# Half as many one-hots on GpSimd, and one spread of expert numbers for all heads

## The chip, the cores and the metric

The kernel runs on one core of one Trainium2 chip. Times are microseconds (us) of the device for one execution; smaller is better. The core has five engines that run side by side, each through its own list of instructions in a fixed order: TensorE (PE in the profile; PEld is its loading of weights), VectorE (DVE), ScalarE (ACT), GpSimd (POOL) and SyncE (SP, which here only starts transfers). An instruction that waits for data holds up all that stands behind it on its engine. Transfers between the device's memory (HBM) and the core's memory (SBUF) run on 16 DMA engines. GpSimd's queue starts the gathers (transfers by index) and the stores of one-hot sums; SyncE's queue starts the rest.

## The reference, cut to what matters

One layer of a streaming encoder on 512 tokens of width 1024. The first sub-layer (attention, an mLSTM, branch gates) is not touched by the change. The second one picks 16 of 16384 single-neuron experts for every token and each of 8 heads:

```python
s = jnp.einsum("thpd,hpnd->thpn", q, sub_keys)
s_top, i_top = lax.top_k(s, PEER_TOPK)
cand = (s_top[:, :, 0, :, None] + s_top[:, :, 1, None, :]).reshape(PEER_BLOCK, PEER_HEADS, 256)
best, ci = lax.top_k(cand, PEER_TOPK)
i1 = jnp.take_along_axis(i_top[:, :, 0, :], ci // PEER_TOPK, axis=-1)
i2 = jnp.take_along_axis(i_top[:, :, 1, :], ci % PEER_TOPK, axis=-1)
e = i1 * N_KEYS + i2
gate = jax.nn.softmax(best, axis=-1)
act = jax.nn.gelu(jnp.einsum("thkd,td->thk", u_exp[e], xb))
return jnp.einsum("thk,thkd->td", (gate * act), v_exp[e])
```

So each token has 128 slots, each with a first expert number, a second one and a gate.

## The kernel before, in words

The 512 tokens are four chunks of 128. The experts of chunk 0 and of the first 32 tokens of chunk 1 are **gathered**: rows of u are fetched by expert number, a dot product with the token on VectorE gives the activation, and (chunk 0 only, in the last stage) rows of v are fetched and summed. All other tokens are done **densely**: for every one of 128 groups of 128 experts TensorE computes the hidden activations of 352 tokens (`hidden`, 24 matmuls from a 512 KB piece of u) and then, in `output`, adds them times v.

The dense way needs, for every token, a 128x128 matrix of gates by first and second number. `build` (line 778) makes it: for one token, `oa` is the one-hot of the first numbers times the gate, `ob` the one-hot of the second numbers, and one matmul `ps_g<-o,oa` (line 801) of the two gives the matrix. It goes in steps of four tokens (`t4`). Per step, `o4` (line 784, VectorE) holds all four `ob`; the four `oa` are shared out: `tt == 1` goes to GpSimd (line 799), `tt == 0` to ScalarE in two instructions (lines 795 and 796, from the 33rd token of chunk 1 on), also `tt == 2` in every fourth step, the rest to VectorE (line 799). ScalarE copies the four results to `gst` (line 802), and after eight steps GpSimd's queue stores 2 MB (`gd<-gst`, line 807). With chunks 2, 3 and 1, in this order, that is 96 steps and 12 stores.

`group` (line 714) serves the 32 gathered tokens of chunk 1. Head by head it forms the expert numbers `et` (line 723, VectorE), spreads them over the 128 partitions by four small transfers to `eg` on SyncE's queue (line 726), and then for four columns gathers a 512 KB tile `ur` of rows of u (line 704, GpSimd's queue) and takes the dot product `junk` (line 712, VectorE): 32 columns in all. `gathered` (line 742) does the same for chunk 0 with 128 columns. Five buffers `ur` are shared by all gathers.

`paced` (line 957) weaves these generators. While `build` takes a step, the side work advances by a rate: `RATE_B` = 0.4 of a `hidden`, `RATE_G` = 0.65 of a step of `group` while chunks 2 and 3 are built, `RATE_0` = 0.8 of a step of `gathered` while chunk 1 is. Between the last head of `scores` and the first build, `TOP` = 2 further `hidden` are called. `group` has a stop after every head's transfers and one after every column: 40 before its end. `slowly` adds that VectorE's part must not be placed ahead of the last `wlo` (line 150, the low half of a weight piece) traced so far.

The program order is not the final one: `schedule_with_timeline_sim` lets a planner simulate the engines with estimated costs when the program is built, and each engine's instructions are lined up as that simulation had them ready. That is why the first heads' `et` stands on VectorE beside the last heads of `scores`.

Of the kernel before, what the change touches and what calls it, by code (L numbers as in the profile page):

```python
# [14 lines left out]
I32 = mybir.dt.int32  # L15
AF = mybir.ActivationFunctionType
ALU = mybir.AluOpType
# [4 lines left out]
P = 128  # L22
# [8 lines left out]
TOPK = 16  # L31
# [8 lines left out]
TG = 32  # L40
NR = P // TG
NJ = TOPK // NR
# [4 lines left out]
LEAD, RA, RB, RC, RG = 1, 2, 1, 1, 2  # L47
ADA_AT, ADA_N = 8, 2
OAP, OAD, TWO = 8, 12, 4
RATE_S, TOP, RATE_G, RATE_B, RATE_0, RATE_A, HOT, COLD = 1.1, 2, 0.65, 0.4, 0.8, 1.0, 2.6, 1.25  # L50
WST, WB, VB = 4, 3, 3

LANES_A = lambda nc: [nc.vector]
# [27 lines left out]
def tile_block(  # L81
# [19 lines left out]
    nc = tc.nc  # L101
# [8 lines left out]
    def bank(tag, name):  # L110
        return psum.tile([P, 512], F32, tag=tag, name=name, bufs=4 if tag == "acc" else 2)
# [52 lines left out]
    def junk():  # L164
        return wpool.tile([P, D], BF16, tag="junk", name="junk", bufs=1)

    state = {"cuts": 2}
# [534 lines left out]
    def row(cp, src, ei, j):  # L702
        t = cp.tile([P, D], F32, tag="ur", name="ur", bufs=UR)
        nc.gpsimd.indirect_dma_start(  # L704
            out=t, out_offset=None, in_=src, in_offset=bass.IndirectOffsetOnAxis(ap=ei[:, j : j + 1], axis=0)
        )
        return t

    def dot_u(cp, ei, j, h2, act):

        t = row(cp, u_r, ei, j)
        nc.vector.scalar_tensor_tensor(  # L712
            junk(), t, 1.0, h2, op0=ALU.mult, op1=ALU.mult, accum_out=act[:, j : j + 1]
        )

    def group(cp):

        slots = state["slots"][:TG, 1]
        eg = cp.tile([P, 8 * NJ], I32, name="eg", bufs=1)
        ag = cp.tile([P, 8 * NJ], F32, name="ag", bufs=1)  # L720
        for h in range(8):
            et = cp.tile([TG, TOPK], I32, tag="et", name="et")
            nc.vector.scalar_tensor_tensor(et, slots[:, 0, h], float(P), slots[:, 1, h], op0=ALU.mult, op1=ALU.add)
            hs = slice(h * NJ, (h + 1) * NJ)
            for g in range(NR):
                nc.sync.dma_start(eg[g * TG : (g + 1) * TG, hs], et[:, g * NJ : (g + 1) * NJ])
            yield
            for j in range(NJ):
                dot_u(cp, eg, h * NJ + j, state["h2"][1], ag)
                yield  # L730
        nc.scalar.activation(ag, ag, AF.Gelu_apprx_tanh)
        at = cp.tile([TG, 8, TOPK], F32, name="at", bufs=1)
        for g in range(NR):
            nc.sync.dma_start(
                at[:, :, g * NJ : (g + 1) * NJ],
                ag[g * TG : (g + 1) * TG, :].rearrange("p (h j) -> p h j", h=8),
            )
        state["at"] = at
        yield

    def gathered(cp, i):

        slots = state["slots"][:, i]
        ei = cp.tile([P, P], I32, name=f"ei{i}", bufs=1)
        nc.vector.scalar_tensor_tensor(
            ei, slots[:, 0].rearrange("p h k -> p (h k)"), float(P), slots[:, 1].rearrange("p h k -> p (h k)"),
            op0=ALU.mult, op1=ALU.add,
        )
        act = cp.tile([P, P], F32, name=f"act{i}", bufs=1)
        yield  # L750
        for j in range(P):
            dot_u(cp, ei, j, state["h2"][i], act)
            yield
        gate = slots[:, 2].rearrange("p h k -> p (h k)")
        nc.scalar.activation(act, act, AF.Gelu_apprx_tanh)
        nc.vector.tensor_mul(act, act, gate)
        yield
        sum_v = cp.tile([P, D], F32, name=f"sum_v{i}", bufs=1)
        for j in range(P):
            t = row(cp, v_r, ei, j)  # L760
            if j == 0:
                nc.vector.tensor_scalar_mul(sum_v, t, act[:, 0:1])
            else:
                nc.vector.scalar_tensor_tensor(sum_v, t, act[:, j : j + 1], sum_v, op0=ALU.mult, op1=ALU.add)  # L764
            yield
        finish(cp, i, (sum_v[:, :512], sum_v[:, 512:]))
        yield

    def build(cp, i, slots):

        ps = bank("g", "ps_slT")
        for j in range(3):
            nc.tensor.transpose(ps[:, j * P : (j + 1) * P], slots[:, j].rearrange("p h k -> p (h k)"), ident)
        sT = cp.tile([P, 3, P], F32, tag="sT", name="sT", bufs=2)
        nc.scalar.copy(sT, ps[:, : 3 * P].rearrange("p (j t) -> p j t", j=3))
        neg = cp.tile([P, 2, P], F32, tag="neg", name="neg", bufs=2)
        nc.scalar.mul(neg, sT[:, 1:, :], -1.0)
        for b in range(P // TB):
            st = cp.tile([P, P, TB], F32, tag="gst", name="gst", bufs=2)
            for t4 in range(TB // 4):  # L780
                ps = bank("gw"[t4 % 2], "ps_g")
                o4 = cp.tile([P, 4, P], F32, tag="two", name="o4", bufs=TWO)
                t0 = b * TB + t4 * 4
                nc.vector.tensor_tensor(
                    out=o4, in0=iota.unsqueeze(1).broadcast_to([P, 4, P]),
                    in1=sT[:, 0, t0 : t0 + 4].unsqueeze(2).broadcast_to([P, 4, P]), op=ALU.is_equal,
                )
                for tt in range(4):
                    t = b * TB + t4 * 4 + tt
                    own = tt == 1  # L790
                    oa = cp.tile([P, P], F32, tag="oap" if own else "oad", name="oa", bufs=OAP if own else OAD)
                    at = sT[:, 1, t : t + 1]
                    gt = sT[:, 2, t : t + 1]
                    if (tt == 0 or (tt == 2 and t4 % 4 == 0)) and i * P + t >= P + TG:
                        nc.scalar.activation(oa, iota, AF.Abs, bias=neg[:, 0, t : t + 1])
                        nc.scalar.activation(oa, oa, AF.Relu, scale=neg[:, 1, t : t + 1], bias=gt)
                    else:
                        e = nc.gpsimd if own else nc.vector
                        e.tensor_scalar(oa, iota, at, gt, op0=ALU.is_equal, op1=ALU.mult)  # L799
                    ob = o4[:, tt]  # L800
                    nc.tensor.matmul(ps[:, tt::4], oa, ob, start=True, stop=True)  # L801
                nc.scalar.copy(
                    st[:, :, t4 * 4 : t4 * 4 + 4],
                    ps.rearrange("p (i t) -> p i t", t=4),
                )
                yield
            nc.gpsimd.dma_start(gd[i * (P // TB) + b], st)
# [77 lines left out]
    def finish(cp, i, halves):  # L885

        if "rows" not in state:
            state["rows"] = [cp.tile([P, D], F32, tag="ur", name=nm, bufs=UR) for nm in ("gt2", "fgb")]
            for t, src in zip(state["rows"], (gtd, final_g)):
                nc.sync.dma_start(t, src.broadcast_to([P, D]))  # L890
        gt2, fgb = state["rows"]
        o = cp.tile([P, D], F32, tag="ur", name="o", bufs=UR)
        xr = cp.tile([P, D], F32, tag="ur", name="xr", bufs=UR)
        nc.sync.dma_start(xr, x2d[i])
        ss = spool.tile([P, 3], F32, tag="ss3", name="ss")
        for n in range(2):
            cs = slice(n * 512, (n + 1) * 512)
            nc.vector.tensor_mul(o[:, cs], halves[n], gt2[:, cs])
            nc.vector.tensor_add(o[:, cs], o[:, cs], xr[:, cs])
            nc.scalar.activation(junk()[:, cs], o[:, cs], AF.Square, accum_out=ss[:, n : n + 1])  # L900
        nc.vector.tensor_add(ss[:, 2:], ss[:, 0:1], ss[:, 1:2])
        rs = spool.tile([P, 1], F32, tag="rs", name="rs")
        nc.scalar.activation(rs, ss[:, 2:], AF.Sqrt, scale=1.0 / D, bias=epst)
        nc.vector.reciprocal(rs, rs)
        for n in range(2):
            cs = slice(n * 512, (n + 1) * 512)
            nc.vector.scalar_tensor_tensor(o[:, cs], o[:, cs], rs, fgb[:, cs], op0=ALU.mult, op1=ALU.mult)
            nc.sync.dma_start(out[i * P : (i + 1) * P, cs], o[:, cs])
# [39 lines left out]
    def slowly(g):  # L948

        while True:  # L950
            with tc.issue_after(state["mark"]):
                ended = next(g, 0) == 0
            if ended:
                return
            yield
# [12 lines left out]
    with pool("epool") as cp:  # L968
# [3 lines left out]
        with pool("dpool") as dp, pool("upool") as up:  # L972
# [9 lines left out]
            for i in (2, 3, 1):  # L982
# [4 lines left out]
                own = (slowly(gather), RATE_0) if i == 1 else (slowly(rows), RATE_G)  # L987
# [79 lines left out]
```

## Time and profile before

| | |
|---|---|
| three runs | 1754.15, 1755.34 (median) and 1758.63 us |
| profiled execution | 1756.35 us, its span 1754.6 us, mean granted clock 0.985 of 2.4 GHz |
| busy share of the span | PE 95%, PEld 83%, DVE 76%, ACT 43%, POOL 41% |
| stages (us from the span's start) | scores end at about 707; builds 707 to 943; remaining `hidden` to 977; `output` to the end |

A stretch of the profile is read by its busy times: an engine that is busy all the time in it sets the pace there, if the others wait for it. The engine that is busy over the whole span need not be the one that paces a stretch. A wait names the instruction that waited and what released it.

### The profile page before, as it was taken

Reading aid. Unit: us, or ns where it says so; the run is one execution under the profiler, and the core shown is the slowest. Engines: PE = TensorE matmul, PEld = TensorE weight load, DVE = VectorE, ACT = ScalarE, POOL = GpSimd, SP = SyncE. Lnnn points to the kernel's source line nnn. Section 1 sums busy time; section 2 is a strip of 40 time slices with the busy share of each in tenths; the row PEclk is TensorE's granted clock in tenths of the full one; section 3 lists DMA queues with packets and bytes.
Section 4 is the critical chain, followed back from the end, with each engine's and each line's share of the span. In section 5 each row is a group of like instructions: output and inputs, shape, how many; then the busy total and the mean of one; then the engine's idle time right before and its main releaser. Section 6 shows DMA issues by size and latency. Waiting matters only on the chain.

```text
span 1754.6 us, 24732 instructions
## 1 busy us (share of the span) xinstructions
PE 1669.1 (95%) x8679; PEld 1448.9 (83%) x8679; DVE 1334.5 (76%) x2732; ACT 756.8 (43%) x1361; POOL 712.6 (41%) x570
## 2 busy tenths in 40 slices
PE   5999999999899998879999999999999999999996
PEld 4766678878788888879999888888888888888885
DVE  7457655675469999778987777787787887787896
ACT  4544544443353333667675433233242333333333
POOL 0000000000147766899996233445345354445450
PEclk9999999999899999999999999999999999999999
DMA  8424234562333336677889998998999989899894
GB/s 300 158 74 137 66 106 134 173 235 96 111 116 102 107 118 210 240 282 299 330 302 385 398 398 317 354 337 317 357 332 333 352 321 370 304 379 338 287 316 161
DMA packets 139613, 440.99 MB, mean 251 GB/s; under 512 B 15489, under 2 KB 42241, under 8 KB 137954
## 3 DMA queue, kind: packets, MB, share of 16 engines
q1 hardware_dynamic: 96290, 263.25, 42.9%
q0 software_dynamic: 43200, 176.18, 27.0%
q8 instruction: 68, 1.11, 0.3%
q14 instruction: 55, 0.45, 0.1%
HBM read 398.05 MB, written 40.90 MB: 250 GB/s over the span
## 4 chain that ended last, share of the span: by engine, by line
PE 50%; DVE 11%; DMA 6%; POOL 3%; issue 3%; ACT 1%; DVEq 0%; SPq 0%; POOLq 0%; ACTq 0%
PE acc L160 10%; PE acc L162 10%; PE acc L161 10%; PE ps_act L162 5%; PE ps_act L160 5%; PE ps_act L161 5%; PE ps_g L801 3%; POOL oa L799 2%; DVE wlo L150 2%; DMA ur<-in_u_r,eg 1%; DMA ur<-in_u_r,ei 1%; DMA wst<-in_u_t 1%; DVE junk L712 1%; DMA vst<-in_v_e 1%; DVE i L648 1%
## 5 line engine op out<-in xcount | busy, mean ns | idle before, releaser
L147 ACT CAST whi<-wst 128x512 fp32r<-128x512 f32 (+1 forms) x300 | 222.6, 773 | 408.0 <-PE ps_act L161 187.7
L162 PE MATMUL ps_act<-h2T_hi,wlo 128*128 128x352 f32 x1024 | 336.8, 329 | 12.5 <-DVE wlo L150 7.3
L160 PE MATMUL ps_act<-h2T_hi,whi 128*128 128x352 f32 x1024 | 333.6, 326 | 0.7 <-ACT ew L815 0.7
L161 PE MATMUL ps_act<-h2T_lo,whi 128*128 128x352 f32 x1024 | 333.8, 326 | 0.0
L150 DVE TENSOR_TENSOR wlo<-wst,whi 128x512 fp32r<-128x512 f32 (+1 forms) x252 | 235.8, 949 | 96.1 <-ACT whi L147 92.7
L161 PE MATMUL acc<-wlo,ehi 128*128 128x512 f32 x768 | 298.6, 390 | 0.0
L162 PE MATMUL acc<-whi,elo 128*128 128x512 f32 x768 | 288.1, 390 | 0.0
L704 POOL DMA_INDIRECT ur<-in_v_r,ei x128 | 191.4, 1496 | 205.0 <-DVE sum_v L764 185.3
L704 POOL DMA_INDIRECT ur<-in_u_r,ei x128 | 183.4, 1433 | 223.1 <-DVE junk L712 210.5
L160 PE MATMUL acc<-whi,ehi 128*128 128x512 f32 x768 | 263.9, 391 | 2.0 <-ACT ehi L866 2.0
L712 DVE SCALAR_TENSOR_TENSOR junk<-ur,h 128x1024 bf16<-128x1024 f32 x160 | 197.0, 1231 | 45.0 <-DMA ur<-in_u_r,eg 28.2
L162 PEld LDWEIGHTS ps_act<-h2T_hi,wlo 128*128 128x128 f32 x1024 | 194.6, 190 | 19.4 <-DVE wlo L150 10.1
L160 PEld LDWEIGHTS ps_act<-h2T_hi,whi 128*128 128x128 f32 x1024 | 194.5, 190 | 4.9 <-ACT ew L815 1.0
L161 PEld LDWEIGHTS ps_act<-h2T_lo,whi 128*128 128x128 f32 x1024 | 194.7, 190 | 3.9
L147 ACT CAST whi<-vst 128x1024 fp32r<-128x1024 f32 x128 | 132.4, 1048 | 129.7 <-PE acc L162 61.4
L150 DVE TENSOR_TENSOR wlo<-vst,whi 128x1024 fp32r<-128x1024 f32 x128 | 154.7, 1219 | 36.6 <-ACT whi L147 35.9
L764 DVE SCALAR_TENSOR_TENSOR sum_v<-ur,act,sum_v 128x1024 f32<-128x1024 f32 x127 | 162.5, 1280 | 7.5 <-DMA ur<-in_v_r,ei 6.6
L162 PEld LDWEIGHTS acc<-whi,elo 128*128 128x128 f32 x768 | 144.0, 188 | 29.2
L161 PEld LDWEIGHTS acc<-wlo,ehi 128*128 128x128 f32 x768 | 144.2, 188 | 28.3
L160 PEld LDWEIGHTS acc<-whi,ehi 128*128 128x128 f32 x768 | 143.0, 188 | 28.9 <-ACT ehi L866 2.3
L799 POOL TENSOR_SCALAR oa<-iota,sT 128x128 f32<-128x128 f32 x96 | 152.3, 1592 | 1.4
L468 POOL TENSOR_SCALAR_AFFINE_SELECT mbd<-mbc 128x512 f32<-128x512 f32 x4 | 3.1, 768 | 321.9 <-ACT mbc L466 321.9
(302 smaller groups left out, 2861.5 us busy)
## 6 DMA issues: line engine op xcount, KB each, us to landing
wst<-in_u_t SPq DMA_DIRECT2D x128, 512.0 KB
vst<-in_v_e SPq DMA_DIRECT2D x128, 512.0 KB
wst<-in_w_pieces SPq DMA_DIRECT2D x76, 512.0 KB
wst<-in_w_ada SPq DMA_DIRECT2D x48, 512.0 KB
gd<-gst POOLq DMA_DIRECT2D x12, 2048.0 KB
gq<-gd SPq DMA_DIRECT2D x16, 1536.0 KB
ad<-gelu SPq DMA_DIRECT2D x16, 704.0 KB
aq<-ad SPq DMA_DIRECT2D x16, 704.0 KB
```

Source lines behind the costliest of these rows:

```text
L147: nc.scalar.copy(hi[:, cs], t[:, cs])
L150: ins = e.tensor_tensor(out=lo[:, cs], in0=t[:, cs], in1=hi[:, cs].bitcast(F32), op=ALU.subtract)
L160: nc.tensor.matmul(o, a[0], b[0], start=first, stop=False)
L161: nc.tensor.matmul(o, a[0], b[1], start=False, stop=False)
L162: return nc.tensor.matmul(o, a[1], b[0], start=False, stop=last)
L468: nc.gpsimd.affine_select(out=mbd.rearrange("p (q l) -> p q l", q=4), in_=mbc.rearrange("p (q l) -> p q l", q=4), pattern=[[0, 4], [1, P]] ...
L648: nc.vector.max_index(places[:, :8], vals[:, :8], data)
L704: nc.gpsimd.indirect_dma_start(out=t, out_offset=None, in_=src, in_offset=bass.IndirectOffsetOnAxis(ap=ei[:, j : j + 1], axis=0))
L712: nc.vector.scalar_tensor_tensor(junk(), t, 1.0, h2, op0=ALU.mult, op1=ALU.mult, accum_out=act[:, j : j + 1])
L764: nc.vector.scalar_tensor_tensor(sum_v, t, act[:, j : j + 1], sum_v, op0=ALU.mult, op1=ALU.add)
L799: e.tensor_scalar(oa, iota, at, gt, op0=ALU.is_equal, op1=ALU.mult)
L801: nc.tensor.matmul(ps[:, tt::4], oa, ob, start=True, stop=True)
```

## The change

The three lines that differ in kind: which `oa` are GpSimd's, which are ScalarE's, and how the 32 tokens' numbers are spread. Two constants change with them.

```diff
-RATE_S, TOP, RATE_G, RATE_B, RATE_0, RATE_A, HOT, COLD = 1.1, 2, 0.65, 0.4, 0.8, 1.0, 2.6, 1.25
+RATE_S, TOP, RATE_G, RATE_B, RATE_0, RATE_A, HOT, COLD = 1.1, 3, 0.62, 0.4, 0.8, 1.0, 2.6, 1.25
...
-    def dot_u(cp, ei, j, h2, act):
-
-        t = row(cp, u_r, ei, j)
-        nc.vector.scalar_tensor_tensor(
-            junk(), t, 1.0, h2, op0=ALU.mult, op1=ALU.mult, accum_out=act[:, j : j + 1]
-        )
+    def dots_u(cp, ei, n, h2, act):
+
+        for j in range(n):
+            nc.vector.scalar_tensor_tensor(
+                junk(), row(cp, u_r, ei, j), 1.0, h2, op0=ALU.mult, op1=ALU.mult, accum_out=act[:, j : j + 1]
+            )
+            yield
...
         slots = state["slots"][:TG, 1]
+        et = cp.tile([TG, 8, TOPK], I32, name="et", bufs=1)
+        nc.vector.scalar_tensor_tensor(et, slots[:, 0], float(P), slots[:, 1], op0=ALU.mult, op1=ALU.add)
         eg = cp.tile([P, 8 * NJ], I32, name="eg", bufs=1)
         ag = cp.tile([P, 8 * NJ], F32, name="ag", bufs=1)
-        for h in range(8):
-            et = cp.tile([TG, TOPK], I32, tag="et", name="et")
-            nc.vector.scalar_tensor_tensor(et, slots[:, 0, h], float(P), slots[:, 1, h], op0=ALU.mult, op1=ALU.add)
-            hs = slice(h * NJ, (h + 1) * NJ)
-            for g in range(NR):
-                nc.sync.dma_start(eg[g * TG : (g + 1) * TG, hs], et[:, g * NJ : (g + 1) * NJ])
-            yield
-            for j in range(NJ):
-                dot_u(cp, eg, h * NJ + j, state["h2"][1], ag)
-                yield
+        for g in range(NR):
+            nc.sync.dma_start(
+                eg[g * TG : (g + 1) * TG, :].rearrange("p (h j) -> p h j", h=8), et[:, :, g * NJ : (g + 1) * NJ]
+            )
+        yield
+        yield from dots_u(cp, eg, 8 * NJ, state["h2"][1], ag)
...
-                    own = tt == 1
+                    own = tt == 1 and t4 % 2 == 0
...
-                    if (tt == 0 or (tt == 2 and t4 % 4 == 0)) and i * P + t >= P + TG:
+                    if (tt == 0 or (tt == 2 and t4 % 2)) and i * P + t >= P + TG:
```

GpSimd now makes the `oa` of the second token of every other step. ScalarE makes a second `oa` in every other step (the odd ones) in place of every fourth. VectorE makes the rest. `et` is one instruction that needs the slots of all eight heads, followed by four transfers. `group` now has 33 stops before its end.

## Rows read from the trace of the kernel before

**Rows 1.** The page's first two parts: busy time, share of the span and instructions of each engine, and the span in 40 slices (tenths busy).

```profile
PE 1669.1 (95%) x8679; PEld 1448.9 (83%) x8679; DVE 1334.5 (76%) x2732; ACT 756.8 (43%) x1361; POOL 712.6 (41%) x570
...
PE   5999999999899998879999999999999999999996
...
POOL 0000000000147766899996233445345354445450
```

**Rows 2.** Busy time of each engine by stretch. Columns: the stretch, its length, busy time and count of PE, PEld, DVE, ACT and POOL, mean granted clock, share of the DMA engines, GB/s.

```profile
669.00:697.00 28.00, 23.79 (x143) 22.64 (x142) 28.00 (x87) 11.78 (x18) 15.15 (x12) 1.00 0.65 216
697.00:707.00 10.00, 8.86 (x58) 8.57 (x57) 7.43 (x10) 4.23 (x6) 6.63 (x4) 1.00 0.96 335
707.00:787.00 80.00, 65.89 (x457) 64.06 (x457) 60.69 (x125) 55.68 (x128) 75.55 (x50) 0.96 0.71 251
787.00:866.00 79.00, 73.11 (x511) 72.47 (x511) 68.05 (x140) 58.58 (x135) 74.60 (x55) 0.93 0.82 305
866.00:943.00 77.00, 74.91 (x544) 74.14 (x543) 71.64 (x147) 55.75 (x121) 72.87 (x54) 1.00 0.89 329
...
1100.00:1400.00 300.00, 300.00 (x1482) 262.44 (x1481) 238.14 (x286) 104.07 (x124) 131.38 (x92) 1.00 0.93 341
```

**Rows 3.** All waits of PE from 980 us to the end of `output` (1745 us): total us, times, longest.

```profile
PE acc L160 <- ACT ehi L866: 2.0, 1, 2.0
PE ps_act L160 <- ACT ew L815: 0.7, 1, 0.7
```

**Rows 4.** Waits in the builds, 707 to 943 us.

```profile
DVE junk L712 <- DMA ur<-in_u_r,eg: 26.1, 5, 7.5
...
PE ps_g L801 <- DVE o L784: 11.4, 4, 4.9
ACT gst L802 <- DMA gd<-gst: 10.6, 2, 6.6
...
PE ps_g L801 <- POOL oa L799: 8.4, 5, 2.8
...
DVE junk L712 <- DMA ur<-in_u_r,ei: 5.3, 1, 5.3
```

**Rows 5.** GpSimd's instructions in order of time: start, length, what ran. First the stretch around one head of the gathered tokens, then one of the build of chunk 1.

```profile
707.34 0.97 POOL L704 DMA_INDIRECT ur<-in_u_r,eg  x1 [3.08 <-DMA eg<-et]
...
712.89 20.52 POOL L799 TENSOR_SCALAR oa<-iota,sT 128x128 f32<-128x128 f32 x12
733.57 1.02 POOL L704 DMA_INDIRECT ur<-in_u_r,eg  x1 [0.16 <-issue]
...
796.22 26.45 POOL L799 TENSOR_SCALAR oa<-iota,sT 128x128 f32<-128x128 f32 x16
822.83 1.02 POOL L704 DMA_INDIRECT ur<-in_u_r,eg  x1 [0.16 <-issue]
...
910.61 1.45 POOL L704 DMA_INDIRECT ur<-in_u_r,ei  x1 [0.16 <-issue]
912.10 1.58 POOL L799 TENSOR_SCALAR oa<-iota,sT 128x128 f32<-128x128 f32 x2
913.84 1.01 POOL L704 DMA_INDIRECT ur<-in_u_r,ei  x1 [0.17 <-issue]
```

**Rows 6.** Groups of instructions in the builds, 707 to 943 us: line, engine, operation, tiles, shapes, count, busy us, mean ns of one, idle before.

```profile
L799 POOL TENSOR_SCALAR oa<-iota,sT 128x128 f32<-128x128 f32 x96 | 152.3, 1592 | 1.4
...
L712 DVE SCALAR_TENSOR_TENSOR junk<-ur,h 128x1024 bf16<-128x1024 f32 x49 | 59.7, 1219 | 31.6 <-DMA ur<-in_u_r,eg 26.1 <-DMA ur<-in_u_r,ei 5.3
L799 DVE TENSOR_SCALAR oa<-iota,sT 128x128 f32<-128x128 f32 x178 | 59.2, 364 | 0.0
...
L796 ACT ACTIVATE oa<-oa,sT,neg 128x128 f32<-128x128 f32 x110 | 52.4, 491 | 0.1
...
L795 ACT ACTIVATE oa<-iota,neg 128x128 f32<-128x128 f32 x110 | 42.5, 400 | 22.9 <-PE ps_g L801 22.3
...
L704 POOL DMA_INDIRECT ur<-in_u_r,ei x26 | 36.2, 1392 | 5.3 <-issue 3.7 <-DVE oa L799 1.2 <-DVE junk L712 0.3
```

**Rows 7.** The one-hots `oa` on GpSimd alone, by build: stretch, length, GpSimd's busy time and count, clock, DMA.

```profile
707.00:787.00 80.00, 56.62 (x32) 0.96 0.71 251
787.00:866.00 79.00, 50.96 (x33) 0.93 0.82 305
866.00:943.00 77.00, 44.70 (x32) 1.00 0.89 329
```

**Rows 8.** Line 799 on GpSimd: durations in ns, smallest, median and largest, first and last start.

```profile
L799 POOL TENSOR_SCALAR oa<-iota,sT x96: 782/1362/4519, 712.9 to 934.6; 128x128 f32<-128x128 f32 x96
```

**Rows 9.** VectorE in order of time, at the end of `scores`: two of the six early dot products with what they cost, `et` of the second head, and the reduction that completes the last head's slots.

```profile
685.14 3.24 DVE L712 SCALAR_TENSOR_TENSOR junk<-ur,h 128x1024 bf16<-128x1024 f32 x1
...
689.45 0.16 DVE L723 SCALAR_TENSOR_TENSOR et<-slots 32x16 int32<-32x16 f32 x1
...
704.04 1.30 DVE L712 SCALAR_TENSOR_TENSOR junk<-ur,h 128x1024 bf16<-128x1024 f32 x1 [2.05 <-DMA ur<-in_u_r,eg]
...
705.27 1.21 DVE L700 TENSOR_REDUCE slots<-m 128x64 f32<-128x1024 f32 x1
```

**Rows 10.** From the chain of waits that ended last, 700 to 1300 us: a gather of rows of u that is on it (start, length).

```profile
697.55 10.67 DMA ur<-in_u_r,eg
```

**Rows 11.** GpSimd in order of time: its first gather for the second head of the 32 tokens (start, length; in brackets its wait and what ended it).

```profile
694.37 1.23 POOL L704 DMA_INDIRECT ur<-in_u_r,eg  x1 [7.07 <-DMA eg<-et]
```

More of the change, by code (lines that the diff above doesn't have):

```diff
@@ L750, in gathered @@
         yield
-        for j in range(P):
-            dot_u(cp, ei, j, state["h2"][i], act)
-            yield
+        yield from dots_u(cp, ei, P, state["h2"][i], act)
         gate = slots[:, 2].rearrange("p h k -> p (h k)")
```

## The prediction

> **What bounds the kernel now.** I read the busy shares first: PE 95%, no other engine over 76% [rows 1]. Then PE's waits after 980 us: 2.7 us in 765 [rows 3], with PE busy all the time from 1100 on [rows 2]. So whatever PE saves ahead of 980 us arrives at the end, and nothing gained on VectorE or GpSimd behind it counts. Then the slices: GpSimd is at eight and nine tenths only in slices 17 to 20 of 40 [rows 1], 702 to 877 us; by stretches these lie in the builds, where POOL is busy 75.55 of 80, 74.60 of 79 and 72.87 of 77 us [rows 2]. PE has 65.89, 73.11 and 74.91 there, VectorE 60.69, 68.05 and 71.64. So in the first two builds GpSimd sets the pace, and in the third all three engines are near full.
>
> The waits say how GpSimd does it. PE waits 8.4 us for one-hots from GpSimd and 11.4 us for `o` from VectorE; VectorE has waited 26.1 us for gathered rows `ur<-in_u_r,eg`, and its one-hots stand behind those dot products [rows 4]. The gathers are late because they stand on GpSimd behind one-hots: 12 of them, 20.52 us, then the next head's gather; 16 of them, 26.45 us, then the next [rows 5]. In the third build, where the gathers of chunk 0 need no spreading per head, GpSimd alternates two one-hots and one gather [rows 5].
>
> From 669 us (where the first `et` is made) to 943 us, 274 us in all, PE is busy 23.79 + 8.86 + 65.89 + 73.11 + 74.91 = 246.6 us and VectorE 28.00 + 7.43 + 60.69 + 68.05 + 71.64 = 235.8 us [rows 2]. PE's idle 27.4 us is the stake.
>
> **One-hots.** 96 steps of four tokens make 384 `oa`. Before: GpSimd 96, ScalarE 110, VectorE 178 [rows 6]. After: GpSimd 48; ScalarE 88 (one in each of the 88 steps from token 160 on) and 44 (one more in the odd ones), 132; VectorE 384 - 48 - 132 = 204.
> - GpSimd loses 48 x 1.592 = 76.4 us of its 223 in the builds [rows 2, 6]. Even with the eight gathers that come in below (8 x 1.392 = 11 us [rows 6]) it has about 158 us of work there and is no longer the bound.
> - ScalarE gains 22 x (0.400 + 0.491) = 19.6 us [rows 6]. It is busy 170 of the builds' 236 us [rows 2]; with 190 it stays under VectorE and PE, so I cost it at nothing; if that cover were gone it is at most the 19.6 us.
> - VectorE gains 26 x 0.364 = 9.5 us [rows 6]. This is on the path once VectorE is full.
>
> **Expert numbers at once.** Seven `et` (0.16 us each [rows 9]) and 28 small transfers go: about 1.1 us of VectorE. What weighs more is that the first `et` now needs the last head's slots, complete at 705.27 + 1.21 = 706.5 us [rows 9]. Eight gathers and six dot products that ran before 707 move behind it. The six are taken out of the last selections, where VectorE is busy 28.00 of 28 us [rows 2]: the two shown cost 3.24 and 2.05 + 1.30 us [rows 9], the other four some 1.2 us each (mean 1.219 [rows 6]), 11.4 us together. So the slots are complete up to 11 us earlier, at best at 695. The dot products come back in the builds, so in the sum over 669 to 943 they cancel. Queued behind the new wait: on SyncE the four transfers, on GpSimd the first gathers with the one-hots behind them, on VectorE the first dot product, and for that PE waits. From the first gather of a head back to its `et` it took 694.37 - 689.45 = 4.9 us, and one gather from issue to use 10.67 us [rows 9 to 11]: some 16 us from `et` to the first dot product. The planner has `o4`, one-hots and three `hidden` to put ahead of that dot product, so I take nothing for it; without the cover it is 16 us once, where now there are five waits of 26.1 us in sum [rows 4]. Below nothing I bound it by those 26.1 us going altogether.
>
> **Constants.** One `hidden` more before the builds is one less behind them: no change in PE's work; either way it is at most the 24 matmuls of one `hidden`, 3.5 us by the first build's 65.89/457 us per matmul [rows 2]. `group` stops 33 times; at 0.62 it is through after 55 of the 64 steps, before 41 of 64 x 0.65 = 41.6 were just enough. That brings the 32 columns no later at their end, so I take nothing.
>
> **The sum.** Two floors for the stretch of 274 us. PE: 246.6 us of work at the share of the third build, 74.91/77 = 0.973, gives 253.5 us, 20.5 less. VectorE: 235.8 + 9.5 - 1.1 = 244.2 us at its share in the third build, 71.64/77 = 0.930, gives 262.5 us, 11.5 less [rows 2]. The longer one counts: VectorE takes over as the bound, and 11.5 us are gained. 1756.35 - 11.5 = 1744.9 in the profiled execution; the median of the runs is 1.0 us below that execution, so 1744.
>
> **A rule weighed.** A one-hot on GpSimd takes 782 ns at best, 1362 in the median and 4519 at worst [rows 8]; the work is the same each time, so something holds it. The Trainium skill (SBUF — State Buffer, "SBUF: two separate sides") says that VectorE and GpSimd share a pair of ports under an exclusive lock, and that the loser is blocked for a whole instruction. By that rule a fuller VectorE makes each remaining GpSimd instruction longer. The trace agrees with the spread but not with the growth: the mean falls from 56.62/32 = 1.77 over 1.54 to 1.40 us while VectorE's busy share rises from 0.76 over 0.86 to 0.93 [rows 2, 7]. So the sum keeps 1.592, and the rule's outcome is rival D.
>
> **Rivals.**
> A, PE sets the pace: the planner packs VectorE better than in the third build, and the gain is PE's 20.5 us, 1735. For it: the granted clock of 0.96 and 0.93 in the first two builds against 1.00 in the third [rows 2] could come back too, 0.04 x 80 + 0.07 x 79 = 8.7 us, 1726 at best. Against it: VectorE's 244 us in 253 would be 96% busy.
> B, no change: PE waits for VectorE's one-hots in place of GpSimd's, and the waits for rows are shared out instead of going. VectorE's 38.2 us of idle [rows 2] shrink only by what it gains in work, 8.4 us; 274 us stay 274, 1755.
> C, slower: the rows are late for another reason than GpSimd's queue (10.67 us from issue to use [rows 10], five buffers), so VectorE's 38.2 us of idle stay in full and its added 8.4 us are paid on top: 1764. For it: the gathers start at one point, behind one wait, and 32 instead of 24 fall in the first two builds. Against it: the long runs of one-hots ahead of the late gathers [rows 5]. It decides where VectorE's waits for `ur` up to the end of the builds stay over some 30 us.
> D, GpSimd held off: its other work in 669 to 943 is 244.8 - 152.3 = 92.5 us [rows 2, 6], so in 262 us there is room for 48 one-hots of 3.5 us. At the worst duration 48 x 4.519 + 92.5 = 309 us, 35 more than now, 1790. Against it: the falling means [rows 7].
> E, the change does not do what it says: the planner's order can put the gathers in bursts again. That ends as B and is in its chance.
>
> **Chances.** Forecast 0.52, A 0.15, B with E 0.18, C 0.12, D 0.03. A measurement of this kernel can tell 0.3% from no change, 5.3 us. Faster by over that is the forecast without its weaker end and A: 0.65. Within: B and that end, 0.20. Slower: C and D, 0.15. The range goes from A with part of the clock, 1729, to just under C, 1761; it leaves out D, most of C and A's last end. The forecast's own range is 1736 to 1750.
>
> **What would show it.** Right: in the builds GpSimd 48 one-hots and under 75% busy; waits of VectorE for `ur<-in_u_r,eg` well under 26 us; PE's waits for `oa` from GpSimd and for `o` together under 8 us against 19.8; `output` starting some 11 us earlier and lasting as long as now. The last selection ends some 10 us earlier, and one longer wait of VectorE stands at the first dot product. Wrong: `output` starts earlier but lasts longer (the gain is given back), or VectorE idles over 30 us waiting for rows (C), or the mean one-hot on GpSimd is over 3 us (D).

## The result and the profile after

The changed kernel takes 1743.53 us (median of four runs, 1740.86 to 1746.01) against 1755.17 before: a ratio of 0.993, with a 95% interval of 0.9909 to 0.9951. The forecast was 1744 with a range of 1729 to 1761. The time is right; of the way there, one half is right and one half is not.

The page's first two parts, for the changed kernel:

```profile
PE 1664.5 (96%) x8679; PEld 1446.8 (83%) x8679; DVE 1342.4 (77%) x2750; ACT 769.4 (44%) x1406; POOL 632.5 (36%) x524
...
POOL 0000000000147765957483234444434434444450
```

GpSimd has lost 80 us of work against [rows 1], and the row of nines in its slices is gone. The span is 15.5 us shorter in this execution. PE has 4.6 of them in busy time (1669.1 to 1664.5, at a mean granted clock of 0.985 in both) and 10.9 in idle time.

Busy times by stretch of the changed kernel (columns as in [rows 2]):

```profile
669.00:707.00 38.00, 33.38 (x203) 31.94 (x203) 34.77 (x90) 22.01 (x46) 24.80 (x14) 0.96 0.50 165
707.00:787.00 80.00, 74.90 (x543) 74.74 (x542) 72.48 (x148) 67.27 (x160) 58.58 (x42) 0.98 0.82 303
787.00:866.00 79.00, 78.01 (x551) 77.48 (x550) 66.38 (x128) 56.07 (x125) 42.36 (x37) 1.00 0.99 384
866.00:943.00 77.00, 76.01 (x551) 75.82 (x551) 74.72 (x157) 61.79 (x132) 49.26 (x37) 1.00 0.86 324
943.00:985.00 42.00, 32.43 (x176) 31.09 (x175) 26.47 (x33) 13.73 (x20) 13.59 (x11) 0.88 1.03 392
```

From 669 to 943 us PE is now busy 262.3 of 274 us, where it was 246.6: 15.7 us gained, and GpSimd is at 64% in the builds. But the last stretch is new: PE idles 9.6 of 42 us at a mean clock of 0.88, where it was busy 41.3 of these 42 us before.

The waits of PE, then of VectorE, from 669 to 943 us:

```profile
PE ps_g L798 <- DVE o L781: 5.1, 1, 5.1
...
PE ps_g L798 <- DVE oa L796: 1.0, 1, 1.0
```

```profile
DVE junk L712 <- DMA ur<-in_u_r,eg: 11.5, 2, 7.3
...
DVE slots L983 <- DMA at<-ag: 2.9, 1, 2.9
```

PE's waits for one-hots and for `o` went from 19.8 us [rows 4] to 6.1, none of them for GpSimd, and VectorE's waits for the 32 tokens' rows from 26.1 us [rows 4, from 707 us on] to 11.5, of which 7.3 is the first.

The builds did not end sooner. PE's matmuls of one-hots, first in the kernel before, then in the changed one (shortest, median and longest in ns, first and last start):

```profile
L801 PE MATMUL ps_g<-o,oa x768: 270/275/550, 714.0 to 941.5; 128*128 128x128 f32 x192
...
L798 PE MATMUL ps_g<-o,oa x768: 270/275/488, 700.3 to 940.1; 128*128 128x128 f32 x192
```

The first build starts 14 us sooner, the last ends where it did. The reason is a gap ahead of chunk 1. VectorE in order of time:

```profile
839.37 0.59 DVE L796 TENSOR_SCALAR oa<-iota,sT 128x128 f32<-128x128 f32 x2
...
842.28 1.23 DVE L712 SCALAR_TENSOR_TENSOR junk<-ur,h 128x1024 bf16<-128x1024 f32 x1
...
862.04 0.28 DVE L983 TENSOR_TENSOR slots<-slots,at 32x128 f32<-32x128 f32 x1 [2.87 <-DMA at<-ag]
...
866.88 0.69 DVE L781 TENSOR_TENSOR o<-iota,sT 128x512 f32<-128x512 f32 x1 [0.52 <-ACT sT L772]
```

The last one-hots of chunk 3 are made at 840 us. Chunk 1 cannot start, because its gates are first multiplied by the activations of its 32 gathered tokens; the last of their dot products is at 842.28 us, the transfers of the activations (`at<-ag`) take some 14 us, and the first `o` of chunk 1 follows at 867 us. PE fills the gap with `hidden`: the trace counts 1065 matmuls `ps_act` from 669 to 943 us where there were 926, six `hidden` more. That is how PE's saved idle time arrives: not as an earlier end of the builds, but as work that is already done. The output stage's first matmul comes at 982.4 us instead of 994.0 (one of its three kinds of matmul, first the kernel before, then the changed one):

```profile
L160 PE MATMUL acc<-whi,ehi x768: 387/389/494, 994.0 to 1740.5; 128*128 128x512 f32 x192
...
L160 PE MATMUL acc<-whi,ehi x768: 387/389/398, 982.4 to 1724.7; 128*128 128x512 f32 x192
```

It would have come sooner still, but when the `hidden` ran out, the output stage's loads were not there. From the chain of waits from 930 us on:

```profile
941.26 12.00 DMA gd<-gst
...
953.84 21.00 DMA vst<-in_v_e
...
982.60 1.39 PE acc L160 x6
```

### The profile page after: what moved, and what is told of

It is laid out like the page before. It is cut to its first block, busy times and chain, and to the rows that moved or that the text cites. A ratio compares the mean times of both kernels' runs of the same rounds, so it can differ in the third digit from the quotient of the medians.

```text
span 1739.1 us, 24668 instructions
## 1 busy us (share of the span) xinstructions
PE 1664.5 (96%) x8679; PEld 1446.8 (83%) x8679; DVE 1342.4 (77%) x2750; ACT 769.4 (44%) x1406; POOL 632.5 (36%) x524
## 4 chain that ended last, share of the span: by engine, by line
PE 55%; DVE 10%; DMA 3%; POOL 3%; issue 2%; ACT 0%; SPq 0%; DVEq 0%; POOLq 0%; ACTq 0%
PE acc L160 10%; PE acc L162 10%; PE acc L161 10%; PE ps_act L160 7%; PE ps_act L162 7%; PE ps_act L161 7%; PE ps_g L798 3%; DMA vst<-in_v_e 1%; DVE wlo L150 1%; POOL oa L796 1%; DMA ur<-in_u_r,eg 1%; DVE i L648 1%; DVE sc L649 1%; DVE i L651 1%; DMA gd<-gst 1%
## 5 line engine op out<-in xcount | busy, mean ns | idle before, releaser
L704 POOL DMA_INDIRECT ur<-in_v_r,ei x128 | 185.1, 1446 | 209.3 <-DVE sum_v L761 191.2
L160 PE MATMUL acc<-whi,ehi 128*128 128x512 f32 x768 | 252.7, 391 | 0.0
L712 DVE SCALAR_TENSOR_TENSOR junk<-ur,h 128x1024 bf16<-128x1024 f32 x160 | 195.4, 1221 | 19.9 <-DMA ur<-in_u_r,eg 11.5
L863 ACT CAST ehi<-gq 128x768 fp32r<-128x768 f32 x64 | 53.4, 837 | 233.4 <-PE acc L161 199.9
L150 POOL TENSOR_TENSOR wlo<-wst,whi 128x512 fp32r<-128x512 f32 x50 | 67.3, 1361 | 163.3 <-ACT whi L147 163.3
```

Source lines behind the costliest of these rows:

```text
L150: ins = e.tensor_tensor(out=lo[:, cs], in0=t[:, cs], in1=hi[:, cs].bitcast(F32), op=ALU.subtract)
L160: nc.tensor.matmul(o, a[0], b[0], start=first, stop=False)
L704: nc.gpsimd.indirect_dma_start(out=t, out_offset=None, in_=src, in_offset=bass.IndirectOffsetOnAxis(ap=ei[:, j : j + 1], axis=0))
L712: nc.vector.scalar_tensor_tensor(junk(), row(cp, u_r, ei, j), 1.0, h2, op0=ALU.mult, op1=ALU.mult, accum_out=act[:, j : j + 1])
L863: nc.scalar.copy(whb, w)
```

## The experiments

Ratios are to the kernel before, timed beside each run on the same chip; there it took between 1755.6 and 1758.4 us, so ratios are compared and not times. "Seam" is 943 to 985 us, where the builds meet the output stage. "Chunk 1 starts" with PE's first matmul of its one-hots, at 873.5 us in the kernel before and 870.2 in the changed one.

**The parts, one at a time.** The new sharing of the one-hots in the kernel before:

```diff
-                    own = tt == 1
+                    own = tt == 1 and t4 % 2 == 0
...
-                    if (tt == 0 or (tt == 2 and t4 % 4 == 0)) and i * P + t >= P + TG:
+                    if (tt == 0 or (tt == 2 and t4 % 2)) and i * P + t >= P + TG:
```

> The kernel before with the new sharing of the one-hots alone (GpSimd 48, ScalarE 132, VectorE 204); expert numbers head by head and the constants as before. Theory G (GpSimd's one-hots are what delays the gathers): most of the change's 11.6 us comes here, a time of 1743 to 1749; VectorE's waits for rows of the 32 tokens in the builds fall from 26.1 to under 15 us. Theory S (the spread head by head is what puts the gathers in bursts): 1752 to 1757, the waits stay above 20 us, and at most 4 us are gained.

1749.11 us, 0.9946 (0.9926 to 0.9966): 9.3 us less than the kernel before beside it, and at the edge of theory G's range. VectorE's waits for the tokens' rows, and the busy times from 669 to 943 us:

```profile
DVE junk L712 <- DMA ur<-in_u_r,eg: 14.2, 4, 5.1
```

```profile
669.00:943.00 274.00, 259.67 (x1812) 256.55 (x1813) 255.40 (x568) 205.32 (x458) 180.61 (x137) 0.98 0.83 312
```

PE is busy 13.1 us more than before; it waited 8.1 us for one-hots and not at all for `o`, where it was 19.8. Theory G holds.

The spread for all heads in the kernel before (`group` and `dots_u` of the change, one-hots and constants as before):

```diff
+        nc.vector.scalar_tensor_tensor(et, slots[:, 0], float(P), slots[:, 1], op0=ALU.mult, op1=ALU.add)
...
+        yield from dots_u(cp, eg, 8 * NJ, state["h2"][1], ag)
```

> The kernel before with the expert numbers of all heads at once alone; one-hots and constants as before. Theory G: GpSimd still has 152 us of one-hots, stays above 90% busy in the builds, and the time is 1752 to 1758. Theory S: the gathers flow one by one between one-hots as in the third build, VectorE's waits for rows fall under 15 us, and the time is 1743 to 1749.

1759.39 us, 1.000 (0.9984 to 1.0016): nothing, as theory G has it (GpSimd is busy 212.1 of the 236 us from 707 to 943, just under the 90% expected, and the time is 1.4 us over its range). Theory S was right in one point and it did not help: the bursts are gone, and VectorE's waits for the tokens' rows are nearly as short as with the new sharing alone (those for chunk 0's rows rose from 5.3 to 11.7 us). PE got little of it: 3.6 us more busy from 669 to 943 us than before, and 3.7 us less at the seam.

```profile
DVE junk L712 <- DMA ur<-in_u_r,eg: 15.1, 7, 5.5
DVE junk L712 <- DMA ur<-in_u_r,ei: 11.7, 4, 6.1
```

```profile
669.00:943.00 274.00, 250.15 (x1727) 241.75 (x1726) 233.01 (x480) 187.55 (x409) 234.39 (x169) 0.99 0.79 287
943.00:985.00 42.00, 37.62 (x229) 36.39 (x228) 27.90 (x37) 12.82 (x19) 18.74 (x15) 1.00 1.01 398
```

So shorter waits for rows are not a gain by themselves. GpSimd in this kernel, in order of time:

```profile
714.97 5.12 POOL L796 TENSOR_SCALAR oa<-iota,sT 128x128 f32<-128x128 f32 x3
720.25 1.10 POOL L704 DMA_INDIRECT ur<-in_u_r,eg  x1 [0.16 <-issue]
721.39 4.21 POOL L796 TENSOR_SCALAR oa<-iota,sT 128x128 f32<-128x128 f32 x2
725.76 1.59 POOL L704 DMA_INDIRECT ur<-in_u_r,eg  x1 [0.17 <-issue]
```

Gathers and one-hots alternate, with no free time between them: the last gather for the 32 tokens was issued at 841.6 us, in the kernel before, with its bursts [rows 5], at 826.7.

Both without the two constants:

```diff
-RATE_S, TOP, RATE_G, RATE_B, RATE_0, RATE_A, HOT, COLD = 1.1, 3, 0.62, 0.4, 0.8, 1.0, 2.6, 1.25
+RATE_S, TOP, RATE_G, RATE_B, RATE_0, RATE_A, HOT, COLD = 1.1, 2, 0.65, 0.4, 0.8, 1.0, 2.6, 1.25
```

> The changed kernel with TOP = 2 and RATE_G = 0.65 as before. If the constants carry nothing, as the prediction took it: 1741 to 1747. If the hidden that TOP moves ahead of the builds covers the first wait for rows: PE idles some 4 us more at the start of the builds and the time is 1747 to 1751.

1737.7 us, 0.9882 (0.9861 to 0.9902): outside both expectations, and better than the change. So the two parts together are worth 20.7 us, more than 9.3 and 0 alone. The trace fits a spread that pays once GpSimd has room: the last gather for the 32 tokens is issued at 821.2 us here, at 841.6 with the spread alone. But every one of these edits also changes the order in which the planner lines up the queues, and the next runs show what that alone can do; how much of the 9.3 and of the 20.7 us it is was not told apart. The constants take some of the gain back.

```diff
-RATE_S, TOP, RATE_G, RATE_B, RATE_0, RATE_A, HOT, COLD = 1.1, 2, 0.65, 0.4, 0.8, 1.0, 2.6, 1.25
+RATE_S, TOP, RATE_G, RATE_B, RATE_0, RATE_A, HOT, COLD = 1.1, 3, 0.62, 0.4, 0.8, 1.0, 2.6, 1.25
```

> The kernel before with TOP = 3 and RATE_G = 0.62 alone. If a third hidden ahead of the builds costs by itself: 1.002 to 1.005. If it costs only beside the new spread, whose first gathers come behind it: 0.998 to 1.002.

This is the same pair in the kernel before: 1776.71 us, 1.0115 (1.0095 to 1.0136), far over the first expectation and against the second: 21.1 us lost by two constants that add no work. The last head's `et` is at 831.8 us there instead of 805.2 and chunk 1 starts at 895 instead of 873 us.

**Which constant.** The changed kernel once more, and with one constant put back:

```diff
-RATE_S, TOP, RATE_G, RATE_B, RATE_0, RATE_A, HOT, COLD = 1.1, 3, 0.62, 0.4, 0.8, 1.0, 2.6, 1.25
+RATE_S, TOP, RATE_G, RATE_B, RATE_0, RATE_A, HOT, COLD = 1.1, 2, 0.62, 0.4, 0.8, 1.0, 2.6, 1.25
```

> The changed kernel itself, so that it stands beside the others on one chip: 0.9909 to 0.9951 of the kernel before, as measured.

> The changed kernel with TOP = 2 alone put back, RATE_G = 0.62 kept. With RATE_G = 1.0 the gathers ended as in the changed kernel (825.9 against 824.8 us), with both constants put back chunk 1 began 7 us earlier and 20.7 us were gained in place of 12.3. Theory T (TOP is what differs): 0.986 to 0.990 of the kernel before, chunk 1's first step at 860 to 866. Rival R (RATE_G is): 0.991 to 0.995, as the changed kernel, chunk 1's first step at 868 or later.

1744.84 us, 0.9927 (0.9907 to 0.9947), and 1739.09 us, 0.990 (0.9881 to 0.9919), chunk 1 starting at 862.9 us. It is `TOP`: 5.8 us on one chip, with spreads of 1741.16 to 1746.43 and 1735.60 to 1741.51 us. (In the second profile of the changed kernel the builds end at 945.0 us in place of 940.1 and PE is busy 259.1 us from 669 to 943 us in place of 262.3: single readings move by that much from one execution to the next.) GpSimd at the start of the builds shows one part of it; the changed kernel:

```profile
694.72 14.05 POOL L796 TENSOR_SCALAR oa<-iota,sT 128x128 f32<-128x128 f32 x8 [2.37 <-ACT sT L772]
708.95 1.18 POOL L704 DMA_INDIRECT ur<-in_u_r,eg  x1 [0.18 <-issue]
```

and the kernel with both constants put back:

```profile
698.69 5.92 POOL L796 TENSOR_SCALAR oa<-iota,sT 128x128 f32<-128x128 f32 x2 [2.37 <-ACT sT L772]
704.78 1.18 POOL L704 DMA_INDIRECT ur<-in_u_r,eg  x1 [0.18 <-issue]
```

With three `hidden` ahead, the planner puts eight one-hots before the first gather, with two only two; the expert numbers had landed by 700.3 us at the latest in the changed kernel (the last of their four transfers was issued at 697.2 us, the slowest of them took 3.1). With `TOP` = 1:

```diff
-RATE_S, TOP, RATE_G, RATE_B, RATE_0, RATE_A, HOT, COLD = 1.1, 3, 0.62, 0.4, 0.8, 1.0, 2.6, 1.25
+RATE_S, TOP, RATE_G, RATE_B, RATE_0, RATE_A, HOT, COLD = 1.1, 1, 0.65, 0.4, 0.8, 1.0, 2.6, 1.25
```

> The changed kernel with TOP = 1 and RATE_G = 0.65. Theory M (each further hidden ahead of the builds holds back the first dot products of the 32 tokens, since they may not go ahead of its wlo): against TOP = 2 the first gather and chunk 1's first step come 3 to 9 us sooner, 0.984 to 0.989. Rival (TOP only reshuffles the planned order, with no trend): anywhere from 0.986 to 0.996, chunk 1's first step not sooner than 860.

1745.26 us, 0.9919 (0.9896 to 0.9942), first gather at 713.6 us, chunk 1 at 875.9, 12.6 us of idle PE at the seam. There is no trend, so theory M falls and its rival stands: `TOP` changes the planned order, for better or worse. Why the planner's order gets worse on either side of 2 was not found.

The rate was tried upward in the changed kernel:

```diff
-RATE_S, TOP, RATE_G, RATE_B, RATE_0, RATE_A, HOT, COLD = 1.1, 3, 0.62, 0.4, 0.8, 1.0, 2.6, 1.25
+RATE_S, TOP, RATE_G, RATE_B, RATE_0, RATE_A, HOT, COLD = 1.1, 3, 1.0, 0.4, 0.8, 1.0, 2.6, 1.25
```

> The changed kernel with RATE_G = 1.0 in place of 0.62, so that the 32 dot products are through after 34 of 64 steps. Theory A (the build of chunk 1 waits for the activations of the 32 tokens, which come 862 us after the start, some 20 us after chunk 3's last one-hot, and the end of the builds at 940 is set by that): the first step of chunk 1 moves from 867 to 850 or earlier, the builds end 10 us or more sooner, PE's 9.6 us of idle between 943 and 980 shrink, and the time is 1732 to 1740. Rival (VectorE is the bound of the whole stretch, so earlier dot products only push one-hots back): chunk 1 may start sooner, the builds end where they did, 1741 to 1747.

1742.73 us, 0.991 (0.9892 to 0.9928). The last gather of the 32 tokens was issued at 825.9 us (824.8 in the changed kernel) and chunk 1 started at 871.4. It tells neither theory from the other, since the rate does not move the gathers.

**What holds chunk 1 back, and what it is worth.** The multiplication by the activations left out of the changed kernel:

```diff
-                    nc.vector.tensor_mul(gate, gate, state["at"])
+                    pass
```

> The changed kernel without the multiplication of the 32 tokens' gates by their activations (left out of the computation), so that nothing of chunk 1's build waits for the 32 dot products; they and their transfers still run. Theory A (chunk 1's build is held back by them from 840 to 867 us, and that sets the end of the builds): the first step of chunk 1 comes before 850, the builds end at 925 or earlier, PE idles under 5 us between them and the output stage, 0.984 to 0.989 of the kernel before. Rival (VectorE's work sets the end of the builds): chunk 1 starts earlier but ends at 935 or later, 0.990 to 0.995.

1739.5 us, 0.9897 (0.9877 to 0.9917), between the two expectations. PE's matmuls of one-hots and the seam:

```profile
L798 PE MATMUL ps_g<-o,oa x768: 270/275/553, 704.1 to 921.8; 128*128 128x128 f32 x192
```

```profile
943.00:985.00 42.00, 35.92 (x205) 34.90 (x205) 30.52 (x40) 15.16 (x21) 15.72 (x12) 0.92 1.03 392
```

Chunk 1's first `o` is at 848.3 us (its matmuls start at 852.0) and the builds end at 922, as theory A has it. But the output stage's first matmul is at 981.6 us, against 982.4 in the changed kernel, and PE still idles 6.1 us at the seam, where theory A had under 5. So the dependence sets where the builds end, and the end of the builds hardly sets the time: 5.3 us came of 18.

The same in a form that leaves nothing out (with `TOP` = 2, `RATE_G` = 0.65): the 32 tokens' block is built last in chunk 1.

```diff
-        for b in range(P // TB):
+        for b in (1, 2, 3, 0) if i == 1 else range(P // TB):
+            if i == 1 and b == 0:
+                pa = bank("g", "ps_at")
+                nc.tensor.transpose(pa[:, :TG], state["at"].rearrange("p h k -> p (h k)"), ident[:TG, :TG])
+                nc.vector.tensor_mul(sT[:, 2, :TG], sT[:, 2, :TG], pa[:, :TG])
...
-                    gate = state["slots"][:TG, 1, 2]
-                    nc.vector.tensor_mul(gate, gate, state["at"])
```

> The changed kernel with both constants put back; the 32 tokens of chunk 1 are built last in it, and their activations are multiplied in after the transpose, so that three quarters of chunk 1's build don't wait for them (nothing left out). If the wait of chunk 1 for the activations costs what it cost with TOP = 3 (3 to 9 us): chunk 1's first step before 850, 0.982 to 0.986. If what is left is set by the loads at the start of the output stage: builds end 10 us or more sooner and the time stays at 0.987 to 0.991.

1735.75 us, 0.9879 (0.9858 to 0.9899): the builds end at 926 instead of 933 us, not quite the 10 us expected, and the time is that of the kernel without this edit (0.9882). The second expectation holds: something at the seam sets the rest.

**Is VectorE the bound?** No one-hot on GpSimd, both constants put back:

```diff
-                    own = tt == 1 and t4 % 2 == 0
+                    own = False
```

> The changed kernel with both constants put back, and no one-hot on GpSimd: VectorE makes 252 where it made 204. Compare with 0.9882, the same without this. Theory V (VectorE is the bound of the builds, as the prediction had it): 48 x 0.364 us = 17 us come on top, 0.995 to 0.999. Theory P (PE is, and fills VectorE's room with hidden work): under 5 us on top, 0.987 to 0.991, and VectorE's busy share in the builds rises above 0.95.

1738.16 us, 0.9889 (0.9871 to 0.9906), against 0.9882 without this edit. VectorE and PE from 669 to 943 us in this kernel:

```profile
669.00:943.00 274.00, 265.06 (x1884) 262.55 (x1883) 259.95 (x571) 213.50 (x467) 95.14 (x78) 1.00 0.86 322
```

48 more one-hots and VectorE is at 95% (259.95 of 274 us, just under the 0.95 expected; 100% in the first build), with PE at 97% as with them on GpSimd (265.56 of 274). The 17 us of theory V are not there: theory P. The run also frees GpSimd of its last one-hots, so a smaller loss at VectorE beside a gain there is not excluded.

**The seam.** Both constants put back, and fewer gathers of chunk 0 around the end of the builds:

```diff
-RATE_S, TOP, RATE_G, RATE_B, RATE_0, RATE_A, HOT, COLD = 1.1, 3, 0.62, 0.4, 0.8, 1.0, 2.6, 1.25
+RATE_S, TOP, RATE_G, RATE_B, RATE_0, RATE_A, HOT, COLD = 1.1, 2, 0.65, 0.4, 0.6, 0.0, 2.6, 1.25
```

> The changed kernel with TOP = 2, RATE_G = 0.65, RATE_0 = 0.6 and RATE_A = 0: fewer gathers of chunk 0 between the builds and the output stage, where the DMA engines are busy all the time. Theory L (PE's idle of 7 to 10 us there is the first loads of the output stage coming late through full DMA engines): under 5 us of idle there, 0.984 to 0.987 of the kernel before. Rival (the loads are late for their place in SyncE's order or for the store ahead of them): idle stays at 7 us or more, 0.987 to 0.991.

1731.54 us, 0.9852 (0.983 to 0.9874), the fastest of all. At the seam, first the kernel with the constants put back, then this one:

```profile
943.00:985.00 42.00, 35.21 (x192) 33.37 (x191) 30.64 (x40) 13.30 (x18) 13.29 (x10) 0.92 1.03 394
```

```profile
943.00:985.00 42.00, 40.66 (x224) 37.40 (x223) 31.10 (x37) 17.61 (x23) 10.63 (x7) 1.00 0.99 368
```

23 instead of 29 gathers had been issued at 940 us, 30 instead of 40 at 985; PE idles 1.3 instead of 6.8 us, the clock does not fall, and the output stage's first matmul is at 962.0 instead of 977.0 us. Theory L's expectations hold. The stage's first load (`gq<-gd`) shows how, with the share of the DMA engines' time that the queues of gathers (`software_dynamic`) and of loads (`hardware_dynamic`) took while it was under way; first the kernel with the constants put back (951 to 975 us):

```profile
950.98 17.24 DMA gq<-gd
```

```profile
q1 hardware_dynamic: 3848, 6.00, 69.6%
q0 software_dynamic: 925, 3.33, 35.4%
```

then this one (945 to 962 us), where no gather is under way (fastest, median and slowest landing of the two `gq` in us; the first is the fastest):

```profile
DMA to landing us min/median/max: 9.0/12.0/14.9
```

```profile
q1 hardware_dynamic: 3709, 5.50, 96.4%
```

The first load lands in 9.0 instead of 17.2 us, which is theory L. It is also issued 5.3 us sooner (945.7 against 951.0 us), behind the last loads for `hidden` in SyncE's order; that part is not told from the rival. The gathers put off are then short at the end. The chain of waits there:

```profile
1695.79 8.40 DMA ur<-in_v_r,ei
1704.28 1.30 DVE sum_v L761
```

The output stage starts 15 us sooner and its last matmul comes 13.4 us sooner, but chunk 0's last rows of v are summed 7 us later than in the kernel with the constants put back (1704.3 against 1697.2 us) and now end the chain: 8.3 us of the span are left.

## Why the prediction was right, and where it was not

**Right: the place and the cause.** GpSimd set the pace of the builds through its queue: with half of its one-hots alone 9.3 us were gained and PE was busy 13.1 us more. PE's and VectorE's waits fell as foreseen (6.1 us under the 8 forecast, 11.5 against 26.1), and the output stage began 11.6 us earlier where 11 was forecast, with nothing given back in it (743 us from its first to its last matmul with 3673 matmuls, before 747 with 3696). One row was read too short: GpSimd's slices at eight and nine tenths are 17 to 21 [rows 1], up to 921 us and not 877, which takes in most of the third build too.

**Right: GpSimd was not held off (rival D).** 48 one-hots took 76.4 us, 1598 ns each, against 1592 before [rows 6], with VectorE busier in the same stretch (248.4 against 235.8 us). The Trainium skill (SBUF — State Buffer, "SBUF: two separate sides") says that the port pair that VectorE and GpSimd share is an exclusive lock. The spread here, 786 to 4851 ns, is what such a lock could make, but the mean again shows no growth, and no run shows what held the long ones.

**Wrong: "VectorE takes over as the bound".** The sum took VectorE's floor, 262.5 us, for the length of the stretch. Its share there was 248.4/274 = 0.906 and not 0.930, and loading it with 48 more one-hots cost nothing that can be told (0.9889 against 0.9882). What counts is the other floor: PE. The mechanism of rival A took place, PE 0.957 busy and 15.7 us gained where A had 20.5, and some of the clock with it (0.98 and 1.00 in the first two builds, before 0.96 and 0.93).

**Wrong: "whatever PE saves ahead of 980 us arrives at the end".** There are 6.9 us of new idle at the seam (2.7 us between the last one-hot and the output stage before, 9.6 after), a term that was not in the sum, and the clock fell to 0.88 there. The output stage's 11.6 us are 15.7 less 6.9, and 2.7 us less of PE's busy time from 669 us to its first matmul for as many matmuls (2004, before 2001), which no run here explains. So the total that came out right is luck: a gain too small and a loss left out, which cancel.

**Wrong: the constants at nothing.** The third `hidden` was counted as PE's work moved, 3.5 us either way. It is not work, it is the planned order that changes: 5.8 us lost on one chip (1744.84 against 1739.09), and 21.1 by both constants in the kernel before. The change is worth 16.5 us with `TOP` alone put back and 20.7 with both constants; the intervals of the two ratios overlap, so what `RATE_G` adds is open.

**Half right: the expert numbers at once.** The slots were complete 12.9 us earlier (their last reduction started at 692.4 us instead of 705.27 [rows 9]), where 11 was forecast. The first wait was not fully covered: VectorE stood 7.3 us for the first gather and PE 5.1 us for the `o` behind it, inside the bound of 16. What was not seen is what the spread is for in the sum: alone nothing, beside the relieved GpSimd some 11 us (20.7 less 9.3), the planner's order included.

**Not seen: chunk 1's wait.** That the 32 columns come "no later at their end" held for the last gather (issued at 824.8 us, before at 826.7) but not for what follows it: the gates of chunk 1 are multiplied at 862.0 us, before at 857.9. It should have been read as a limit: chunk 1 cannot begin before them, so the builds could not end earlier. Leaving the multiplication out showed that this sets their end, and that it is worth only some 5 us, since PE has other work to put there.

**What would have shown it in the trace of before.** The stretch between 943 and 985 us in the kernel before (columns as in [rows 2]):

```profile
943.00:985.00 42.00, 41.32 (x257) 40.80 (x256) 24.32 (x31) 14.28 (x20) 17.06 (x13) 1.00 1.02 414
```

The DMA engines are full, with PE busy because `hidden` were left to do. Of the idle time taken out ahead of this place, 6.9 of 15.7 us were handed to the loads behind it.

## What to carry to other kernels

Where a queue is shared by compute and by transfers, thin out the compute first: here spreading the transfers evenly was worth nothing while the queue was full and some 11 us once it wasn't. When one engine's wait goes and another has spare work, the gain appears as work done early: look for where that work runs out and which loads must be there by then. A constant that only moves work in the program's order is not free where a planner lines up the queues: time it alone.

## What the runs showed of the hardware

- A one-hot of 128x128 on GpSimd took 786 to 4851 ns in the changed kernel and 782 to 4519 ns before [rows 8]. The 14 of the 96 before that met no VectorE instruction took 782 to 805 ns, 793 in the mean; the other 82 took 1729 in the mean, and the longest of them, from 748.07 us, ran beside eight of VectorE's. What holds a one-hot there no run shows.
- Transfers of one size on SyncE's queue took very different times to land. In the changed kernel `eg<-et` and `at<-ag` have 4 KB each (queue, kind, count, size, median us to landing); the third line is `at<-ag` in the fastest kernel:

```profile
eg<-et SPq DMA_DIRECT2D x4, 4.0 KB, 2.3
...
at<-ag SPq DMA_DIRECT2D x4, 4.0 KB, 14.0
...
at<-ag SPq DMA_DIRECT2D x4, 4.0 KB, 5.0
```

  The first went out with the DMA engines half busy (0.50 in 669 to 707 us), the second with them nearly full (0.98 in 841 to 848 us), the third with them little less so (0.93 in the same stretch). So the busy share alone does not tell the time; what else does was not looked into.
- With the idle time at the seam TensorE's clock was granted at 0.72 of 2.4 GHz from 965 to 980 us, that is partly at its lower level of 1.2 GHz, while PE was busy 8.0 of these 15 us; with that idle time gone it stayed at full speed (1.00 at the seam of the fastest kernel). The changed kernel:

```profile
965.00:980.00 15.00, 8.00 (x36) 7.71 (x37) 8.57 (x10) 5.49 (x8) 1.82 (x2) 0.72 1.06 380
```
